# The order of scores, softmax and value products in the attention of a hybrid decoder block

## The chip, the cores and the metric

The kernel runs on one core of one Trainium2 chip. The metric is the device time of one execution in microseconds; the median over runs is compared. TensorE (PE) multiplies, VectorE (DVE), ScalarE (ACT) and GpSimd (POOL) do the rest, and SyncE (SP) issues nearly all DMA transfers.

## The reference

One decoder block on 1024 tokens of width 1024, batch 1, float32. After a norm and an input projection two branches run side by side, and a gated feed-forward layer with a short convolution follows. The change concerns the first branch, an attention with a forget gate in 8 heads of 128 channels:

```python
# log_f: log sigmoid of a forget gate, per token and head
c = jnp.cumsum(log_f, axis=1)
s = einsum('bhqd,bhkd->bhqk', q, k) * 128 ** -0.5
s = s + (c[..., :, None] - c[..., None, :])          # bias of query and key
p = softmax(where(key_pos <= q_pos, s, -inf))
y_fox = einsum('bhqk,bhkd->bhqd', p, v)
```

The second branch, a gated delta rule, is a chunked recurrence: eight chunks of 128 tokens per head, each needing the state that the one before leaves. Both branches are merged by gates, go through an output product and a norm, and then through the feed-forward layer (2816 hidden channels) and a last norm.

## The kernel before, in words

The kernel runs its stages one after the other: norm and input projection (`head_in`, `project`), the two branches together (`mix`, 812 to 1066 us in the profile), the merge (`merge`), the output product (`mix_out`), and the feed-forward layer (`ffn_up`, `ffn_down`). A float32 product is made of three: each operand is cut into a rounded high part and the rest, its low part, and high x high, high x low and low x high are summed. `split` (L106, L107) makes the parts of a tile: ScalarE casts the high part, then VectorE or GpSimd subtracts.

**Attention.** A head's 1024 queries are eight tiles of 128, numbered t; tile t sees (t + 1) x 128 keys. `probs` makes the softmax of one query tile. TensorE multiplies queries and keys into a PSUM bank (L1187 to L1189: the third pair of parts is left out). VectorE adds the bias and keeps the running maximum in one instruction (L1194), once per piece: columns left of the diagonal take the bias row `cr`, those on it the masked copy `cd`. A tile up to t = 3 is one block of scores; a later one is cut in two equal blocks. Then VectorE scales the maximum (L1200), ScalarE takes the exponential with its row sum (L1201), VectorE takes the reciprocal (L1202) and scales the row (L1203). The probabilities stay in SBUF, one tile `p0` to `p7` for each t.

`attend` makes the value products for half of the queries (512). For each key block j TensorE transposes the probability tiles that see it (L1224) into a PSUM bank, ScalarE and VectorE split the result into `ph` and `pl` (L106, L107), and three products add it up in the bank `ya` (L1215). The first half needs the probabilities of tiles 0 to 3, the second half those of tiles 4 to 7. Products run three key blocks behind the transposes.

`fox` orders the heads. For each head it goes through all score tiles, then the first half of the products, then the second. Inside the first half it starts the loads of the next head's queries and keys (`fox_load`, L1119) and its bias row (`fox_bias`, L1148 and L1150); inside the second it issues their split: `fox_query`, `fox_key` (L1135 on ScalarE, L1136 on GpSimd). Queries, keys and bias have one set of tiles in SBUF. The values of a head are loaded at the end of the head before and split by `fox_values` (L1140, L1143, L1144) after tile 4 of the scores. Head 0's tiles 0 to 3 are done early, inside the end of the projection (`fox_first`).

**What sets the order.** Each function is a generator that gives up control at each `yield`; a yield of `fox` is called a step here. A head has 26 steps (12 of scores, 5 and 9 of products), head 0 has 22. `mix` counts these steps as `i` and puts steps of the recurrence between them: `prep(h)` loads and prepares a head of the recurrence, `stream(0)` takes the even heads and `stream(1)` the odd ones, and at every odd `i` from 21 on each stream is advanced by one step. TensorE's instructions are issued in just this order. The order on the other engines and on SP is chosen by a planner that simulates the program while it is built, except for single instructions that are pinned to program order (the casts L1135 and L1143 are). Each engine, SP too, works through its queue in order, so an instruction that waits holds up those behind it.

PSUM has eight banks: in this stage four small ones, shared by scores, transposes and the recurrence (`small`), one for `ya` and three for the recurrence. SBUF pools are stacks from a left and a right end; a pool that is opened where another was closed gets its place, and its first writers wait for the last readers of the old tiles. The pool `stream2` holds the buffers `wr` through which later stages load their weights (`wload`, L126); it is opened ahead of `mix`, at the bottom of the right stack.

Of the kernel before, what the change touches and what calls it, by code (L numbers as in the profile page):

```python
# [17 lines left out]
P = 128  # L18
# [4 lines left out]
H = 8  # L23
# [64 lines left out]
class Block:  # L88
# [322 lines left out]
    def run(self):  # L411
# [5 lines left out]
        with ExitStack() as ctx:  # L417
# [30 lines left out]
            banks(4)  # L448
            self.st = pool(ctx, "stream2", side="right")
            so, sc = ExitStack(), ExitStack()  # L450
# [11 lines left out]

            self.mix([pool(left, f"fox{i}") for i in range(4)], pool(sc, "scan", side="right"), merge_pools)
            sc.close()
# [9 lines left out]
            self.merge(merge_last)  # L474
            bs.close()
            banks(2, 6)
            first = ExitStack()
# [77 lines left out]
    def head_in(self, blk, right):  # L555
# [3 lines left out]
        with tc.tile_pool(name="hin", bufs=1) as pool, ExitStack() as px:  # L559
# [96 lines left out]
            for t in range(NT):  # L656
# [12 lines left out]
                if t == NT - 2:  # L669
# [5 lines left out]
            blk.update(self.blocks(right.enter_context(tc.tile_pool(name="hnt", bufs=1, side="right", reuse_waits="tile")),  # L675
                                   ("t2", "t3", "t1")))
            scalars = self.scalars()
# [445 lines left out]

    def fox_query(self):

        self.fox_parts(self.qh, self.ql)

    def fox_key(self):
        self.fox_parts(self.kh, self.kl)

# [14 lines left out]

    def fox_bias(self, h):
        nc = self.nc
        nc.sync.dma_start(self.cr, self.rows_d[(H + h) * NT:(H + h + 1) * NT, :].rearrange("t c -> (t c)")  # L1148
                          .partition_broadcast(P))
        nc.gpsimd.affine_select(out=self.cd.rearrange("p (n c) -> p n c", n=NT),  # L1150
                                in_=self.cr.rearrange("p (n c) -> p n c", n=NT),
                                compare_op=ALU.is_ge, fill=NEG, base=0, pattern=[[0, NT], [-1, P]],
                                channel_multiplier=1)

    def fox_first(self, pool):

        self.fox_in = pool
        self.qh, self.ql, self.kh, self.kl = (pool.tile([P, S], F32R, name=n) for n in ("qh", "ql", "kh", "kl"))
        self.cr, self.cd = (pool.tile([P, S], F32, name=n) for n in ("cr", "cd"))
        self.vl = pool.tile([P, NT, P], F32R, name="vl")  # L1160
        self.fox_load(self.ql, self.q_d[0])
        self.fox_load(self.kl, self.k_d[0])
        self.fox_bias(0)
        self.fox_load_values(0)
        yield
        self.fox_query()
        yield
        self.fox_key()
        yield
        self.pts = []  # L1170
        for t in range(EARLY):
            yield from self.probs(0, t, self.pts)

    def probs(self, h, t, pts):

        nc, pool, qh, ql, kh, kl = self.nc, self.fox_in, self.qh, self.ql, self.kh, self.kl
        n = (t + 1) * P
        tsl = slice(t * P, n)
        w = n if t < 4 else n // 2
        p = (pool if t < EARLY else self.probs_pool if t < 4 else self.probs_late).tile([P, n], F32, tag=f"p{t}", name=f"p{t}")  # L1180
        mx = pool.tile([P, 4], F32, tag="mx", bufs=4, name="mx")
        top = NEG
        for lo in range(0, n, w):
            sp = self.small()
            sl = slice(lo, lo + max(w, 2 * P))
            o = sp[:, 0:sl.stop - lo]
            nc.tensor.matmul(o, qh[:, tsl], kh[:, sl], start=True, stop=False)  # L1187
            nc.tensor.matmul(o, qh[:, tsl], kl[:, sl], start=False, stop=False)
            nc.tensor.matmul(o, ql[:, tsl], kh[:, sl], start=False, stop=True)  # L1189
            for c0, c1, src in ((lo, min(lo + w, t * P), self.cr), (max(lo, t * P), lo + w, self.cd)):  # L1190
                if c0 >= c1:
                    continue
                i = (c0 > lo) + 2 * (lo > 0)
                nc.vector.tensor_tensor_reduce(p[:, c0:c1], sp[:, c0 - lo:c1 - lo], src[:, c0:c1], 1.0, top,  # L1194
                                               ALU.add, ALU.max, mx[:, i:i + 1])
                top = mx[:, i:i + 1]
            yield
        mm = pool.tile([P, 2], F32, tag="mm", bufs=4, name="mm")

        nc.vector.tensor_scalar(mm[:, 0:1], top, -QSCALE, None, op0=ALU.mult)  # L1200
        nc.scalar.activation(p, p, AF.Exp, bias=mm[:, 0:1], scale=QSCALE, accum_out=mm[:, 1:2])  # L1201
        nc.vector.reciprocal(mm[:, 1:2], mm[:, 1:2])  # L1202
        nc.vector.tensor_scalar(p, p, mm[:, 1:2], None, op0=ALU.mult)  # L1203
        pts.append(p)

    def attend(self, h, half, pts):
# [39 lines left out]
    def fox(self, pools, scan_pool):  # L1246


        self.attend_pool, self.probs_late, values, self.probs_pool = pools
        self.vh = values.tile([P, NT, P], F32R, name="vh")  # L1250
        self.vf = scan_pool.tile([P, 2, P], F32, name="vf")
        self.fox_values()
        for h in range(H):
            pts = [] if h else self.pts
            for t in range(len(pts), NT):
                yield from self.probs(h, t, pts)
                if h and t == 4:
                    self.fox_values()
            for half in range(2):
                for i, _ in enumerate(self.attend(h, half, pts)):  # L1260
                    if h + 1 < H and half == 0:
                        if i == 0:
                            self.fox_load(self.ql, self.q_d[h + 1])
                            self.fox_load(self.kl, self.k_d[h + 1])
                            self.fox_bias(h + 1)
                    elif h + 1 < H:
                        if i == 1:
                            self.fox_query()
                        elif i == 4:
                            self.fox_key()  # L1270
                    yield
            if h + 1 < H:
                self.fox_load_values(h + 1)


    def mix(self, fp, pool, before_last):
        tc, nc, a = self.tc, self.nc, self.a
        self.yf_d, self.yg_d = ([self.dr.tile([P, S], F32, name=f"{n}{h}") for h in range(H)] for n in ("yfd", "ygd"))
        if True:
# [156 lines left out]
            streams = [stream(0), stream(1)]  # L1436
            i = 0
            while take(fox, 1):
                if i in (0, 9):
                    preps[i > 0] = prep(int(i > 0))  # L1440
                if i in (0, 8, 11):
                    take(preps[0], 1)
                elif i in (9, 16, 19):
                    take(preps[1], 1)
                if i >= 21:

                    if i % 2:
# [602 lines left out]
```

## Time and profile before

| | |
|---|---|
| median of 3 runs | 1993.91 us (1989.75 to 1994.09) |
| the profiled execution | 1994.26 us, span 1992.6 us |
| mean clock granted to TensorE | 0.991 |
| TensorE busy | 1920.6 us (96%) |
| VectorE busy | 1492.4 us (75%) |
| ScalarE busy | 1067.5 us (54%) |
| GpSimd busy | 954.3 us (48%) |
| branches together (`mix`) | about 812 to 1066 us |

Times in the profile are counted from the first instruction. A row of a stretch gives the busy time of each engine in it with the number of instructions. A row of a wait reads "who waited, on which tile and line <- for whom: us in all, times, longest". Of matrix products the start is exact and the end is modelled, so the distance between starts tells what one costs when they follow each other. A waiting time put down to an engine belongs to the event that came last.

### The profile page before, as it was taken

To read this page: it belongs to the slowest core of one execution; us is meant where nothing else is said; L and a number is where in the kernel's file an instruction comes from. 1 tells how busy PE (TensorE), PEld (TensorE's weight loads), DVE (VectorE), ACT (ScalarE), POOL (GpSimd) and SP (SyncE) were. 2 spreads that over 40 slices of the span, in tenths; PEclk is the share of its full clock that TensorE was granted. 3 is DMA by queue.
4 is the path that set the end of the run, shared out by engine and by line. 5 is a ranking of instruction groups with operands and counts; after the bars stand their busy time and mean duration, and the time that the engine had idled before them with its cause. 6 is when DMAs were issued, how large, how long until landed. Compare 5 with 4: busy or idle time off the path is not lost. (4 is left out here: it accounts for less than half of the span.)

```text
span 1992.6 us, 29214 instructions
## 1 busy us (share of the span) xinstructions
PE 1920.6 (96%) x9674; PEld 1605.2 (81%) x9674; DVE 1492.4 (75%) x2549; ACT 1067.5 (54%) x2383; POOL 954.3 (48%) x792
## 2 busy tenths in 40 slices
PE   8999999999999999999998999999999999999998
PEld 8988887888887777788886887877788888877886
DVE  6949887867999974487887797668877676778435
ACT  5436776763334445476765443466555555553234
POOL 2845656555555455455655043154665656530012
PEclk9999999999999999899999999999999999999999
DMA  5335556565323366766665743573433434378654
GB/s 166 96 101 164 174 189 188 185 211 206 112 106 111 112 213 257 259 222 212 230 219 203 231 137 131 188 242 124 163 126 112 148 118 136 118 250 319 211 195 160
DMA packets 191608, 350.89 MB, mean 176 GB/s; under 512 B 50784, under 2 KB 79712, under 8 KB 191456
## 3 DMA queue, kind: packets, MB, share of 16 engines
q1 hardware_dynamic: 190448, 345.35, 51.2%
q10 hardware_dynamic: 1008, 3.67, 0.5%
q8 instruction: 76, 1.25, 0.3%
q14 instruction: 76, 0.62, 0.1%
HBM read 232.76 MB, written 116.20 MB: 175 GB/s over the span
## 5 line engine op out<-in xcount | busy, mean ns | idle before, releaser
L107 POOL TENSOR_TENSOR ol<-ws,oh 128x512 fp32r<-128x512 f32 x212 | 288.3, 1362 | 218.4 <-ACT oh L106 207.6
L107 POOL TENSOR_TENSOR ol<-wr,oh 128x512 fp32r<-128x512 f32 x165 | 230.4, 1399 | 271.0 <-ACT oh L106 213.9
L106 ACT CAST oh<-ws 128x512 fp32r<-128x512 f32 x212 | 131.0, 618 | 178.3 <-PE mm L159 172.4
L106 ACT CAST oh<-wr 128x512 fp32r<-128x512 f32 x201 | 121.5, 615 | 107.7 <-PE mm L159 74.2
L205 DVE TENSOR_TENSOR ws<-wr 128x512 f32<-128x512 f32 x106 | 99.1, 935 | 103.2 <-DMA wr<-in_w_up_dram 70.5
L390 DVE SCALAR_TENSOR_TENSOR cv<-c,fw,cv 128x512 f32<-128x512 f32 (+2 forms) x176 | 127.5, 748 | 10.0 <-ACT cv L385 8.5
L390 DVE SCALAR_TENSOR_TENSOR cv<-c,cw,cv 128x511 f32<-128x511 f32 (+2 forms) x144 | 105.9, 748 | 7.4 <-ACT cv L385 5.8
L1038 DVE TENSOR_TENSOR invt<-invz 128x399 f32<-128x399 f32 (+50 forms) x114 | 94.7, 845 | 0.3
L264 ACT COPY x<-mm 128x512 f32<-128x512 f32 x158 | 91.7, 581 | 4.5 <-PE mm L159 4.5
L159 PE MATMUL mm<-b22h,oh 128*128 128x512 f32 x216 | 86.1, 399 | 7.4 <-ACT x L264 7.3
L159 PE MATMUL mm<-bt1h,oh 128*128 128x512 f32 x216 | 85.2, 395 | 5.1 <-ACT x L264 5.1
L107 DVE TENSOR_TENSOR ol<-wd,oh 128x512 fp32r<-128x512 f32 x66 | 46.3, 706 | 57.5 <-ACT oh L106 57.4
L159 PE MATMUL mm<-bt4h,oh 128*128 128x512 f32 x216 | 84.8, 393 | 4.4 <-DVE c L311 4.4
L159 PE MATMUL mm<-b11h,ol 128*128 128x512 f32 x216 | 86.2, 399 | 0.7 <-POOL ol L107 0.7
L159 PE MATMUL mm<-b11h,oh 128*128 128x512 f32 x216 | 85.8, 397 | 1.0 <-ACT oh L106 1.0
L159 PE MATMUL mm<-b11l,oh 128*128 128x512 f32 x216 | 86.4, 400 | 0.0
L159 PE MATMUL mm<-b22l,oh 128*128 128x512 f32 x216 | 86.0, 398 | 0.0
L159 PE MATMUL mm<-b21l,oh 128*128 128x512 f32 x216 | 86.0, 398 | 0.0
L159 PE MATMUL mm<-bt4l,oh 128*128 128x512 f32 x216 | 85.7, 397 | 0.0
L159 PE MATMUL mm<-bt2l,oh 128*128 128x512 f32 x216 | 85.1, 394 | 0.3 <-DVE bt2l L107 0.3
L159 PE MATMUL mm<-bt1l,oh 128*128 128x512 f32 x216 | 84.9, 393 | 0.0
L159 PE MATMUL mm<-b21h,oh 128*128 128x512 f32 x216 | 84.9, 393 | 0.0
(426 smaller groups left out, 6381.0 us busy)
## 6 DMA issues: line engine op xcount, KB each, us to landing
wr<-in_w_up_dram SPq DMA_DIRECT2D x43, 512.0 KB, 3.6
wr<-in_w_gdn_dram SPq DMA_DIRECT2D x24, 512.0 KB, 3.8
wr<-in_w_out_dram SPq DMA_DIRECT2D x24, 512.0 KB, 3.9
s<-hy SPq DMA_DIRECT2D x44, 256.0 KB, 3.0
s<-z SPq DMA_DIRECT2D x44, 256.0 KB, 3.9
wd<-in_w_down_dram SPq DMA_DIRECT2D x44, 256.0 KB, 5.7
b22h<-s SPq DMA_DIRECT2D x44, 256.0 KB, 2.9
b22l<-s SPq DMA_DIRECT2D x44, 256.0 KB, 3.3
```

The source lines that it names most:

```text
L106: cast = nc.scalar.copy(hi, src)
L107: (lo_eng or nc.vector).tensor_tensor(lo, src, hi.bitcast(F32), ALU.subtract)
L159: self.nc.tensor.matmul(ps, lhs[:, sl], rhs[:, k, :], start=(first and k == 0 and i == 0), stop=(k == 3 and i == 2), skip_group_check=True)
L205: v.tensor_tensor(t, x, y, op)
L264: nc.scalar.copy(t, x)
L390: nc.vector.scalar_tensor_tensor(t[:, lo:], c[:, 512 * j + lo - s:512 * (j + 1) - s], w[:, n - 1 - s:n - s], t[:, lo:], op0=ALU.mult, op1= ...
L1038: nc.vector.tensor_tensor(tv, z[:, m:n, 0:n].to_broadcast([P, r, n]), z[:, m, c0:c1].unsqueeze(2).to_broadcast([P, r, n]), ALU.mult))
```

## The change

The change has these parts.

1. `fox` no longer goes through scores, first half and second half in turn. For each head a list gives the order of 26 steps: four times (one step of the first half's products, two score steps of tiles 4 to 7), then the rest of the first half, and the second half's products with the four score tiles 0 to 3 of the next head between them. Since tiles 0 to 3 of a head are always done ahead, as head 0's already were, the first step of each head is a step of products.
2. There are two sets of tiles for queries, keys and the bias row of the first 512 keys (`fox_set`), used by heads in turn. The loads for the next head go out at step 1 of a head, the splits of its queries and keys are issued at steps 6 and 8, that of the head's own values at step 4.
3. The bias row and its masked copy are made in two halves of 512 keys (`fox_bias(h, half)`); the second half's tiles are shared by all heads, and its load goes out after step 12.
4. Scores go in blocks of 512 keys rather than equal halves: tile 4 has now 512 and 128 columns (the second is computed 256 wide), tile 5 512 and 256, tile 6 512 and 384, tile 7 512 and 512 as it was.
5. A score tile of one block gives up control after its softmax rather than before it.
6. `mix` starts the first recurrence head ahead of the first attention step, and the following ones two to three steps earlier.
7. The pool `stream2` is opened after the merge rather than ahead of `mix`, which makes room for the second set; the tiles `t1`, `t2`, `t3` of the projection are laid out in another order.

```diff
-            self.st = pool(ctx, "stream2", side="right")
             so, sc = ExitStack(), ExitStack()
...
-            self.mix([pool(left, f"fox{i}") for i in range(4)], pool(sc, "scan", side="right"), merge_pools)
+            self.mix([pool(left, f"fox{i}") for i in range(5)], pool(sc, "scan", side="right"), merge_pools)
...
             self.merge(merge_last)
             bs.close()
+            self.st = pool(ctx, "stream2", side="right")
...
-                                   ("t2", "t3", "t1")))
+                                   ("t1", "t2", "t3")))
...
+    def fox_bias(self, h, half):
+        nc, n = self.nc, NT // 2
+        cr, cd = self.bias(h, half)
+        r0 = (H + h) * NT + half * n
+        nc.sync.dma_start(cr, self.rows_d[r0:r0 + n, :].rearrange("t c -> (t c)").partition_broadcast(P))
+        nc.gpsimd.affine_select(out=cd.rearrange("p (n c) -> p n c", n=n), in_=cr.rearrange("p (n c) -> p n c", n=n),
                                 compare_op=ALU.is_ge, fill=NEG, base=0, pattern=[[0, n], [-1, P]],
                                 channel_multiplier=1)
+    def bias(self, h, half):
+        return (self.crh if half else self.sets[h % 2][4]), self.cd[half]
+
+    def fox_set(self, pool):
+        return ([pool.tile([P, S], F32R, name=n) for n in ("qh", "ql", "kh", "kl")]
+                + [pool.tile([P, 512], F32, name="crl")])
+
+    def fox_load_head(self, h):
+        _, ql, _, kl, _ = self.sets[h % 2]
+        self.fox_load(ql, self.q_d[h])
+        self.fox_load(kl, self.k_d[h])
+        self.fox_bias(h, 0)
...
     def probs(self, h, t, pts):
...
-        w = n if t < 4 else n // 2
...
-        for lo in range(0, n, w):
+        for half, lo in enumerate(range(0, n, 512)):
             sp = self.small()
-            sl = slice(lo, lo + max(w, 2 * P))
+            hi = min(lo + 512, n)
+            sl = slice(lo, max(hi, lo + 2 * P))
...
-            yield
+            if hi < n:
+                yield
...
         pts.append(p)
+        yield
...
     def fox(self, pools, scan_pool):
...
+            late, early = late(), early()
+            order = [first, late, late] * 4 + [first, early, early, early, last, last, last, early] + [last] * 6
+            for i, part in enumerate(order):
+                if i == 0:
+                    if h == 0:
+                        self.fox_values()
+                elif i == 1 and more:
+                    self.fox_load_head(h + 1)
+                elif i == 4 and h:
                     self.fox_values()
+                elif more and i == 6:
+                    self.fox_query(h + 1)
+                elif more and i == 8:
+                    self.fox_key(h + 1)
+                if next(part, DONE) is not DONE:
                     yield
+                if i == 12:
+                    finish(first)
+                    if more:
+                        self.fox_bias(h + 1, 1)
+            for part in (first, late, early, last):
+                finish(part)
+            if more:
                 self.fox_load_values(h + 1)
+            pts = after
...
     def mix(self, fp, pool, before_last):
...
+            preps[0] = prep(0)
+            take(preps[0], 1)
             while take(fox, 1):
-                if i in (0, 9):
-                    preps[i > 0] = prep(int(i > 0))
-                if i in (0, 8, 11):
+                if i == 6:
+                    preps[1] = prep(1)
+                if i in (5, 8):
                     take(preps[0], 1)
-                elif i in (9, 16, 19):
+                elif i in (6, 14, 17):
                     take(preps[1], 1)
-                if i >= 21:
+                if i >= 19:
...
-                elif i >= 12 and i % 2:
+                elif i >= 9 and i % 2:
                     take(streams[0], 1)
```

More of the change, by code (lines that the diff above doesn't have):

```diff
@@ L1122, in fox_load_values, with fox_query, fox_key @@
         self.fox_load(self.vl, self.vd[:, h * P:(h + 1) * P].rearrange("(t p) d -> p t d", p=P))
[L1124 to L1129, printed above, removed]
+    def fox_query(self, h):
+        self.fox_parts(*self.sets[h % 2][0:2])
+    def fox_key(self, h):
+        self.fox_parts(*self.sets[h % 2][2:4])
     def fox_parts(self, hi, lo):
@@ L1144, in fox_values @@
             self.nc.gpsimd.tensor_tensor(self.vl[:, sl], raw[:, sl], self.vh[:, sl].bitcast(F32), ALU.subtract)
[L1146 to L1152, printed above, removed]
-                                channel_multiplier=1)
+    def fox_bias(self, h, half):
[4 more added lines that the diff above has]
+        nc.gpsimd.affine_select(out=cd.rearrange("p (n c) -> p n c", n=n), in_=cr.rearrange("p (n c) -> p n c", n=n),
+                                compare_op=ALU.is_ge, fill=NEG, base=0, pattern=[[0, n], [-1, P]],
+                                channel_multiplier=1)
@@ L1155, in fox_first @@
+    def bias(self, h, half):
[8 more added lines that the diff above has]
+        self.fox_bias(h, 0)
     def fox_first(self, pool):
         self.fox_in = pool
-        self.qh, self.ql, self.kh, self.kl = (pool.tile([P, S], F32R, name=n) for n in ("qh", "ql", "kh", "kl"))
@@ L1159, in fox_first @@
-        self.cr, self.cd = (pool.tile([P, S], F32, name=n) for n in ("cr", "cd"))
+        self.sets = [self.fox_set(pool)]
+        self.crh = pool.tile([P, 512], F32, name="crh")
+        self.cd = [pool.tile([P, 512], F32, name=f"cd{i}") for i in range(2)]
         self.vl = pool.tile([P, NT, P], F32R, name="vl")
-        self.fox_load(self.ql, self.q_d[0])
-        self.fox_load(self.kl, self.k_d[0])
-        self.fox_bias(0)
+        self.fox_load_head(0)
         self.fox_load_values(0)
+        self.fox_bias(0, 1)
@@ L1165, in fox_first @@
         yield
-        self.fox_query()
+        self.fox_query(0)
         yield
-        self.fox_key()
+        self.fox_key(0)
         yield
@@ L1174, in probs @@
     def probs(self, h, t, pts):
-        nc, pool, qh, ql, kh, kl = self.nc, self.fox_in, self.qh, self.ql, self.kh, self.kl
+        nc, pool, (qh, ql, kh, kl, _) = self.nc, self.fox_in, self.sets[h % 2]
         n = (t + 1) * P
         tsl = slice(t * P, n)
-        w = n if t < 4 else n // 2
-        p = (pool if t < EARLY else self.probs_pool if t < 4 else self.probs_late).tile([P, n], F32, tag=f"p{t}", name=f"p{t}")
+        p = (pool if t < EARLY else self.probs_late).tile([P, n], F32, tag=f"p{t}", name=f"p{t}")
         mx = pool.tile([P, 4], F32, tag="mx", bufs=4, name="mx")
-        top = NEG
-        for lo in range(0, n, w):
+        top, i = NEG, 0
+        for half, lo in enumerate(range(0, n, 512)):
             sp = self.small()
-            sl = slice(lo, lo + max(w, 2 * P))
+            hi = min(lo + 512, n)
+            sl = slice(lo, max(hi, lo + 2 * P))
             o = sp[:, 0:sl.stop - lo]
@@ L1189, in probs @@
             nc.tensor.matmul(o, ql[:, tsl], kh[:, sl], start=False, stop=True)
-            for c0, c1, src in ((lo, min(lo + w, t * P), self.cr), (max(lo, t * P), lo + w, self.cd)):
+            cr, cd = self.bias(h, half)
+            for c0, c1, src in ((lo, min(hi, t * P), cr), (max(lo, t * P), hi, cd)):
                 if c0 >= c1:
                     continue
-                i = (c0 > lo) + 2 * (lo > 0)
-                nc.vector.tensor_tensor_reduce(p[:, c0:c1], sp[:, c0 - lo:c1 - lo], src[:, c0:c1], 1.0, top,
+                nc.vector.tensor_tensor_reduce(p[:, c0:c1], sp[:, c0 - lo:c1 - lo], src[:, c0 - lo:c1 - lo], 1.0, top,
                                                ALU.add, ALU.max, mx[:, i:i + 1])
-                top = mx[:, i:i + 1]
-            yield
+                top, i = mx[:, i:i + 1], i + 1
+            if hi < n:
+                yield
         mm = pool.tile([P, 2], F32, tag="mm", bufs=4, name="mm")
@@ L1246, in fox @@
     def fox(self, pools, scan_pool):
-        self.attend_pool, self.probs_late, values, self.probs_pool = pools
+        self.attend_pool, self.probs_late, values, other, _ = pools
         self.vh = values.tile([P, NT, P], F32R, name="vh")
         self.vf = scan_pool.tile([P, 2, P], F32, name="vf")
-        self.fox_values()
+        self.sets.append(self.fox_set(other))
+        pts = self.pts
         for h in range(H):
[L1254 to L1257, printed above, removed]
-                    self.fox_values()
[L1259 to L1270, printed above, removed]
-                    yield
-            if h + 1 < H:
@@ new lines, in fox, with late, early @@
+            more, after = h + 1 < H, []
+            first, last = self.attend(h, 0, pts), self.attend(h, 1, pts)
+            def late():
+                for t in range(4, NT):
+                    yield from self.probs(h, t, pts)
+            def early():
+                for t in range(4 if more else 0):
+                    yield from self.probs(h + 1, t, after)
+            late, early = late(), early()
+            order = [first, late, late] * 4 + [first, early, early, early, last, last, last, early] + [last] * 6
```

## The prediction

> **What bounds the kernel now.** I read the page first, then the table of stretches, the waits of TensorE, and the order of time around two heads.
>
> ```profile
> PE 1920.6 (96%) x9674; PEld 1605.2 (81%) x9674; DVE 1492.4 (75%) x2549; ACT 1067.5 (54%) x2383; POOL 954.3 (48%) x792
> ```
>
> TensorE is busy for 96% of the span, so a change can give back only the time in which it waits, or runs at a lower clock. The change touches the attention stage alone. The next rows are the first head there, then the sum over the six heads from 843.0 to 1036.4 us, then the last head (columns: stretch, its length, busy time of each engine, granted clock, DMA share, GB/s; a sum row ends in means).
>
> ```profile
> 811.90:843.00 31.10, 27.13 (x178) 22.86 (x176) 18.94 (x54) 15.11 (x34) 15.66 (x14) 0.84 0.97 334
> sum 193.42, PE 182.70 PEld 166.59 DVE 156.62 ACT 134.67 POOL 112.95; mean PE 30.45 PEld 27.77 DVE 26.10 ACT 22.44 POOL 18.82
> 1036.40:1065.40 29.00, 26.79 (x189) 24.11 (x187) 22.65 (x87) 22.00 (x69) 9.98 (x12) 1.00 0.39 135
> ```
>
> Six heads take 193.4 us, 32.2 each, of which TensorE idles 10.7 in all. The first head loses 31.1 - 27.1 = 4.0 us idle, and its mean clock of 0.84 costs up to 0.16 x 31.1 = 5.0 more. The last head idles 2.2. These 21.9 us are the ceiling. VectorE has 26.1 us of work in a head of 32.2: enough room over a head, if it is spread. It isn't: one head, cut where the last score goes out.
>
> ```profile
> 904.36:918.00 13.64, 12.72 (x91) 11.88 (x89) 12.93 (x57) 9.73 (x35) 4.89 (x5) 1.00 0.47 142
> 918.00:937.30 19.30, 17.98 (x135) 15.80 (x135) 13.39 (x38) 13.18 (x40) 10.10 (x9) 1.00 0.95 316
> ```
>
> While TensorE does scores, VectorE is busy for 12.9 of 13.6 us; in the value products for 13.4 of 19.3. It still falls behind, as three moments of this head show (start, length, engine, line):
>
> ```profile
> 916.38 0.40 PE L1189 MATMUL ms<-kh,ql 128*128 128x512 f32 x1
> 923.97 0.75 DVE L1203 TENSOR_SCALAR p<-p,mm 128x1024 f32<-128x1024 f32 x1
> 924.78 0.33 PE L1224 MATMUL ms<-ident,p 128*128 128x128 f32 x1 [0.71 <-DVE p L1203]
> ```
>
> The last score is issued at 916.4, its tile is normalised 7.6 us later, and the transpose that needs it waits. TensorE's waits in the six heads say the same (us in all, times, longest):
>
> ```profile
> PE ya L1215 <- DVE pl L107: 3.7, 3, 2.0
> PE ms L1224 <- DVE pl L107: 1.8, 3, 1.2
> PE ms L1224 <- DVE p L1203: 1.8, 3, 0.7
> PE ms L1224 <- DVE mx L1194: 1.0, 1, 1.0
> ```
>
> 8.3 of the 10.7 us are waits for VectorE.
>
> **The change, part by part.** *Order of scores and products.* A head has 26 steps of TensorE: 12 of scores, then 14 of products. Afterwards the first twelve hold the eight score steps of tiles 4 to 7 and four steps of the first half; the other fourteen the rest of the products and the four early tiles of the next head. What this does to VectorE comes from these rows (the first is L1194 alone, the rest groups over the six heads; us in all, mean ns):
>
> ```profile
> 843.00:1036.00 193.00, 48.16 (x228) 1.00 0.63 214
> L1203 DVE TENSOR_SCALAR p<-p,mm 128x128 f32<-128x128 f32 (+7 forms) x48 | 34.0, 708 | 0.1
> L1202 DVE RECIPROCAL mm<-mm 128x1 f32<-128x1 f32 x48 | 7.3, 153 | 0.7 <-ACT p L1201 0.6
> L1200 DVE TENSOR_SCALAR mm<-mx 128x1 f32<-128x1 f32 x48 | 6.6, 140 | 0.1
> L107 DVE TENSOR_TENSOR pl<-ms,ph 128x512 fp32r<-128x512 f32 (+2 forms) x60 | 35.7, 605 | 12.9 <-ACT ph L106 12.3
> ```
>
> Softmax costs VectorE (48.16 + 34.0 + 7.3 + 6.6) / 6 = 16.0 us a head, the low parts of the transposed tiles 35.7 / 6 = 5.95. Of 26.1 that leaves 4.2 for the scans (overlaps counted off), by steps 1.9 in twelve and 2.3 in fourteen. The early tiles have 1280 of 4608 columns (28%, 4.4 us) and half of the tiles (8.0 us); I take 5.0, nearer the columns, since most of L1203 and L1194 grows with width. The first half has 10 of 36 transposes: 1.65 of 5.95. So the score steps hold now 16.0 + 1.9 = 17.9 us of VectorE against 12.7 of TensorE, an excess of 5.2; afterwards 11.0 + 1.65 + 1.9 = 14.5, an excess of 1.8 (TensorE's 12.7 left as it is: the early scores leave, transposes and two products come). The fourteen others get 5.0 + 4.3 + 2.3 = 11.6 against some 18. If waits shrink with the excess, 1.8 / 5.2 = 35% stays: **-7.0 us** of 10.7 in six heads, **-1.4** of 2.2 in the last. Ends: nothing, and all 12.9.
>
> *The start.*
>
> ```profile
> 811.90:828.50 16.60, 13.55 (x79) 10.70 (x78) 12.60 (x42) 7.60 (x16) 7.22 (x6) 0.80 0.95 361
> 820.90 0.41 PE L1224 MATMUL ms<-ident,p 128*128 128x128 f32 x2 [1.06 <-DVE mx L1194]
> 822.24 0.48 PE L1224 MATMUL ms<-ident,p 128*128 128x128 f32 x1 [0.93 <-DVE pl L107]
> 823.37 0.63 PE L1215 MATMUL ya<-ph,vl 128*128 128x512 f32 x1
> 816.99 1.10 SPq L126 DMA_DIRECT2D wr<-in_w_out_dram  x2
> ```
>
> Head 0 has the same eight score steps and four of products in its first 16.6 us, with 12.6 of VectorE in them. These stay; TensorE's four transposes can now fill the gaps, so at best the stretch shrinks to 12.6: **-4.0 us**, between nothing and the whole 9.0. Waits of about 1 us were enough here for half speed: 823.37 follows at 0.42 us spacing and longer. The Trainium skill ("TensorE: Matmul & The Clock Gate", Part 1) has the clock fall after an idle window of about 3.4 us; no wait here is that long, so the trace does not agree. By that rule only the 4.0 idle us are to be had, at the same share 1.8, and the sum would be 2.2 smaller.
>
> *Blocks of 512 keys.* Tile 4 goes from 320 + 320 to 512 + 256 columns; the others keep theirs.
>
> ```profile
> 915.92 0.39 PE L1187 MATMUL ms<-kh,qh 128*128 128x512 f32 x1
> 916.15 0.40 PE L1188 MATMUL ms<-kl,qh 128*128 128x512 f32 x1
> ```
>
> 512 columns go out every 0.23 us, so 128 more in three products cost 0.17 us, in eight heads **+1.4**. VectorE loses one reduction of 192 columns a head (in the excess above, under 0.4 us; not counted).
>
> *Second set of queries and keys.* These loads had to wait on SP for the last scores, and now need not:
>
> ```profile
> SPq L1119 <- PE ms L1188: 27.9, 5, 8.9
> ```
>
> No TensorE wait in the six heads names them, so I cost this at nothing; it is the condition for the new order. Their casts stay pinned on ScalarE, from steps 18 and 21 to 6 and 8; behind them stand the exponentials and the high parts of the transposes.
>
> *Bias by halves.* One more 256 KB load and one more select a head; POOL's select of 1024 columns (below) costs between the same and twice as much: 0 to 1.1 us a head on an engine busy 18.8 of 32.2. Nothing on the path.
>
> *The weight stream's tiles* (three loads of 512 KB that went out at 817.0) open after the merge. They leave the start's full DMA (share 0.97; part of the start's bounds) and enter the merge, long before the output product at about 1250. I take 0. If they delay the merge's loads, 1.5 MB at the 334 GB/s above is +4.7; that is the upper end. The reorder of three tiles moves addresses alone: 0.
>
> **Sum:** -7.0 - 1.4 - 4.0 + 1.4 = -11.0. The profiled execution took 1994.3 us (span 1992.6), 0.4 over the median, so 1983.3. Ends: -21.9 + 1.4, 1973.8; and 0 + 1.4 + 4.7, 2000.4. For the forecast itself, 1977 to 1988.
>
> **Rivals.** *VectorE stays the bound.* POOL's low parts come under the late normalisations now:
>
> ```profile
> 914.57 2.55 POOL L1144 TENSOR_TENSOR vl<-vl,vh 128x512 fp32r<-128x512 f32 x2 [5.59 <-ACT vh L1143]
> 915.93 1.53 DVE L1203 TENSOR_SCALAR p<-p,mm 128x640 f32<-128x640 f32 x1
> 919.85 0.60 DVE L1203 TENSOR_SCALAR p<-p,mm 128x768 f32<-128x768 f32 x1
> ```
>
> 640 columns took 1.53 us beside POOL, 768 took 0.60 without. If all four late tiles pay 0.93, that is 3.7 us a head; the mean of 708 ns over the eight widths, against about 0.45 at 0.60's pace, shows some 1.0 paid already on four. With 2.7 more the excess is 4.5 of 5.2, 87% of each wait stays, and the sum is -0.13 x (12.9 + 4.0) + 1.4 = -0.8: 1993.5. Against it: VectorE's own order is chosen by a planner, not by the file. The Trainium skill ("SBUF — State Buffer", Who interferes with whom) states the rule behind this: VectorE and GpSimd share a port pair under an exclusive lock, and the later one blocks wholly. The rows agree. The planner could also keep VectorE's old order, and then the change doesn't do what it says; the time is the same.
>
> *More than forecast:* all waits and the lost clock go, 1974 to 1977. For it: the fourteen other steps have over 6 us of spare VectorE. Against it: some waits are chains, not load.
>
> *Slower: the next head's low parts come late.* Place: the first early score, at step 13. The key's low part starts after step 8, behind the values' and the query's, in the same twelve steps:
>
> ```profile
> L1144 POOL TENSOR_TENSOR vl<-vl,vh 128x512 fp32r<-128x512 f32 x12 | 16.4, 1383 | 19.1 <-ACT vh L1143 19.0
> L1136 POOL TENSOR_TENSOR ql<-ql,qh 128x512 fp32r<-128x512 f32 x12 | 15.2, 1287 | 8.5 <-ACT qh L1135 8.5
> L1136 POOL TENSOR_TENSOR kl<-kl,kh 128x512 fp32r<-128x512 f32 x12 | 15.2, 1287 | 1.7 <-ACT kh L1135 1.7
> L1150 POOL TENSOR_SCALAR_AFFINE_SELECT cd<-cr 128x1024 f32<-128x1024 f32 x6 | 6.6, 1094 | 19.5 <-DMA cr<-rows 19.5
> ...
> 782.82 0.39 PE L1188 MATMUL ms<-kl,qh 128*128 128x256 f32 x1 [2.77 <-POOL kl L1136]
> ```
>
> That is (16.4 + 15.2 + 15.2 + 6.6) / 6 = 8.9 us of POOL in a burst, with waits for loads between. A step takes 32.2 / 26 = 1.24 us, so from step 8 to 13 there are 6.2 us; it decides when the key's low part ends later than that. Such a wait costs 2.77 us (head 0's first score); in seven heads 19.4, and -11.0 + 19.4 gives 2002.7. Against it: the old order left four steps after the key's cast, the new one five, without such a wait between heads.
>
> **How the numbers follow.** Forecast 0.40; more than forecast 0.14; VectorE stays the bound, 1988 to 2000, 0.26; late low parts, above 2000, 0.20. 0.3% (6 us) is about what a measurement of this kernel can tell from no change: below 1988 is faster, 0.40 + 0.14 + 0.02 of the third = 0.56; 0.24 the same; 0.20 slower. The range leaves out 0.03 below 1975 and 0.15 above 2003.
>
> **What would show it.** Right: the stretch from the first transpose to the last value product falls by 8 to 14 us, VectorE's busy share becomes even over a head, waits of L1224 and L1215 for L107, L1203 and L1194 fall below 6 us, and TensorE's clock near 820 to 830 is above 0.8. Wrong: L1203's mean grows well over 708 ns; L1188 or L1215 wait for POOL; the merge after 1066 waits longer for its loads.

## The result, and the profile after

The changed kernel takes **2025.62 us** (median of four runs, 2023.3 to 2029.17), the kernel before 1992.18 on the same occasions: ratio 1.017, 95% interval 1.0149 to 1.0191. It is slower by some 33 us, and the predicted range ended at 2003.

The profiled execution took 2025.05 us, span 2023.3, 30.8 us more than that of before. The page's first part (busy time, share, instructions) already says that the number of products did not grow: 9674 as before, which take 10 us longer.

```profile
PE 1930.7 (95%) x9674; PEld 1611.0 (80%) x9674; DVE 1489.6 (74%) x2533; ACT 1072.0 (53%) x2383; POOL 961.1 (48%) x800
```

The attention stage is cut here in three, in both kernels at the same events: its start, the eviction of the second half's sums (`ye`) of head 0, that of head 6, and the merge's first product. The columns are those of the prediction's stretches. After:

```profile
811.00:848.50 37.50, 31.89 (x211) 27.33 (x210) 26.04 (x83) 20.25 (x54) 18.30 (x17) 0.86 1.00 325
848.50:1067.10 218.60, 192.69 (x1383) 172.80 (x1382) 156.57 (x540) 135.64 (x433) 113.66 (x124) 0.95 0.56 184
1067.10:1097.70 30.60, 24.80 (x152) 22.27 (x150) 19.91 (x56) 20.57 (x57) 13.60 (x16) 0.89 0.26 87
```

Before:

```profile
811.90:843.80 31.90, 27.93 (x184) 23.66 (x183) 19.25 (x55) 15.61 (x36) 16.46 (x15) 0.84 0.95 327
843.80:1037.20 193.40, 182.68 (x1380) 166.57 (x1379) 156.69 (x553) 134.56 (x432) 112.15 (x120) 1.00 0.64 215
1037.20:1067.70 30.50, 26.24 (x182) 23.38 (x180) 24.41 (x90) 23.90 (x75) 10.38 (x14) 1.00 0.41 135
```

The stage is 286.7 us long instead of 255.8, which is the whole difference. The six heads in the middle have nearly the same work (tile 4's blocks are wider) and take 25.2 us more. TensorE idles 25.9 us in them instead of 10.7, and its products take 10.0 us longer, at a mean granted clock of 0.95. The first stretch now holds the early tiles of head 1 as well, and the last one lacks such tiles, so these two are compared together: 68.1 against 62.4 us.

TensorE's waits in the six heads after (us in all, times, longest):

```profile
PE ya L1232 <- ACT vh L1143: 11.7, 3, 6.5
PE ya L1232 <- POOL vl L1144: 5.4, 4, 1.5
PE ms L1204 <- POOL ql L1136: 4.8, 1, 4.8
PE ms L1203 <- POOL kl L1136: 2.0, 1, 2.0
PE us L1386 <- DVE sr L1383: 0.9, 3, 0.4
PE us L1381 <- DVE ss L1398: 0.8, 1, 0.8
```

VectorE, which 8.3 us of waits named before, is down to 1.7 us. In its place stand 17.1 us for the parts of the **values** (L1143 is the cast to the high part, L1144 the subtraction of the low part) and 6.8 us for those of queries and keys. The last two rows are products of the recurrence.

The longest of them, in order of time. TensorE (start, length, engine, line):

```profile
990.34 0.39 PE L1232 MATMUL ya<-pf,vf 128*128 128x128 f32 x2
...
999.33 0.27 PE L1241 MATMUL ms<-ident,p 128*128 128x128 f32 x1
1006.05 0.80 PE L1232 MATMUL ya<-ph,vh 128*128 128x512 f32 x1 [6.45 <-ACT vh L1143]
1006.64 0.63 PE L1232 MATMUL ya<-pl,vh 128*128 128x512 f32 x1
```

SP's queue at that time, and ScalarE's cast:

```profile
989.55 0.47 SPq L1320 DMA_DIRECT2D sat<-a21d  x1
...
994.78 0.63 SPq L1320 DMA_DIRECT2D sqd<-qdd  x1
995.52 0.56 SPq L1261 DMA_DIRECT2D yfd<-ye  x1
996.21 0.37 SPq L1119 DMA_DIRECT2D vl<-vd  x1
```

```profile
1005.38 1.14 ACT L1143 CAST vh<-vl 128x512 fp32r<-128x512 f32 x2 [2.65 <-DMA vl<-vd]
```

At a head's last product, 990.3, the one tile of the loaded values is free. The load of the next ones goes out at 996.2, behind ten loads of the recurrence and a store; ScalarE has them at 1005.4, and the next head's first product follows at 1006.1. TensorE was ready for it at 999.6, 9.3 us after the last product. In the old order the same chain had more room (TensorE and SP, before):

```profile
937.15 0.39 PE L1215 MATMUL ya<-pf,vf 128*128 128x128 f32 x2
954.00 0.47 PE L1215 MATMUL ya<-ph,vh 128*128 128x512 f32 x1
```

```profile
936.49 0.38 SPq L1119 DMA_DIRECT2D vl<-vd  x1
```

There the first product came 16.9 us after the last. By steps: the old order has 15 from a head's last product to the next one's first (twelve of scores, then three key blocks of transposes), the new one nine. The chain of 990.3 to 1006.1 took 15.7 us; it fits into the one and not into the other.

That is the longest of the three waits for the cast, and the only one that ends on the load. In head 1 the load went out at 847.9 and landed 8.0 us later, when TensorE was ready (856.2); but ScalarE had an exponential and the cast of the next head's key ahead, and cast the values at 859.7, which made TensorE wait for 4.2 us. In head 6 the data were there at 1036.5 and the cast came at 1042.4, behind an exponential, copies and half of the key's cast; the wait was 1.05 us. In heads 3 and 4 the values were in time. So ScalarE's order belongs to the chain too.

The second kind of wait, on GpSimd (start, length) with TensorE's row behind it:

```profile
895.99 2.82 POOL L1144 TENSOR_TENSOR vl<-vl,vh 128x512 fp32r<-128x512 f32 x2
...
900.93 2.52 POOL L1136 TENSOR_TENSOR kl<-kl,kh 128x512 fp32r<-128x512 f32 x2
903.40 2.42 POOL L1422 TENSOR_TENSOR so<-so,srs 128x512 f32<-128x512 f32 x2
905.88 0.52 POOL L1342 MEMSET sxt<- 64x512 f32 x1
906.48 2.82 POOL L1136 TENSOR_TENSOR ql<-ql,qh 128x512 fp32r<-128x512 f32 x2
```

```profile
908.12 0.58 PE L1204 MATMUL ms<-kh,ql 128*128 128x256 f32 x1 [4.75 <-POOL ql L1136]
```

GpSimd works through values, key and query and the recurrence's own tiles without a gap, and the first early score stands for 4.75 us: the slower rival's wait, at its place. It comes in two of the six heads, here for the query and once, 2.0 us, for the key, and in head 0 (2.8 us).

### The profile page after: what moved, and what is told of

The parts are those of the page before. It is cut to its first block, busy times and chain, and to the rows that moved or that the text cites. A ratio compares the mean times of both kernels' runs of the same rounds, so it can differ in the third digit from the quotient of the medians.

```text
span 2023.3 us, 29182 instructions
## 1 busy us (share of the span) xinstructions
PE 1930.7 (95%) x9674; PEld 1611.0 (80%) x9674; DVE 1489.6 (74%) x2533; ACT 1072.0 (53%) x2383; POOL 961.1 (48%) x800
## 5 line engine op out<-in xcount | busy, mean ns | idle before, releaser
L159 PE MATMUL mm<-bt2h,oh 128*128 128x512 f32 x216 | 84.4, 391 | 1.8 <-ACT x L264 1.8
```

Of the source, the lines that this page charges most:

```text
L159: self.nc.tensor.matmul(ps, lhs[:, sl], rhs[:, k, :], start=(first and k == 0 and i == 0), stop=(k == 3 and i == 2), skip_group_check=True)
```

## The experiments

Theory A: what costs is the values. One buffer, free only after a head's last product, must be loaded and split in nine steps. Theory B, the prediction's slower rival: the burst of low parts on GpSimd. Theory C: something else of the change. Ratios are to the kernel before on the same chip; what an edit gives back is counted as the difference of two ratios, 0.1% being 2 us, and is uncertain by some 6 us where four runs were made. One kernel's runs spread over 10 us (the kernel before: 1989.2 to 1999.4 in 13), and in the traces the stage starts between 805.5 and 816.4 us though the edits hardly touch the code ahead of it. So the stage's own length in the trace is given beside the time: 286.7 us after, 255.8 before. Line numbers move by a few lines from kernel to kernel.

**The old order.** The changed kernel with the old order of steps, and with the steps of loads and splits that suit it; everything else as changed.

```diff
-            order = [first, late, late] * 4 + [first, early, early, early, last, last, last, early] + [last] * 6
+            order = [late] * 8 + [first] * 5 + [last] * 9 + [early] * 4
```

(loads at step 8, values split at 2, query and key at 14 and 17)

> The changed kernel with the list of steps put back to the order of the kernel before: eight score steps of tiles 4 to 7, five steps of the first half, nine of the second, then the four early tiles of the next head; loads at step 8, values' parts at step 2, queries' and keys' parts at steps 14 and 17. Two sets of queries and keys, bias by halves, blocks of 512 and the later weight pool stay. If the new order of steps is what costs (first theory), the time comes back to 1990 to 1998 us. If the rest of the change costs (other addresses, weight pool, blocks, bias loads), it stays above 2010.

2000.6 us, ratio 1.0027 (1.0013 to 1.0041), stage 261.0 us: just above the first theory's range and far below the other's. The order and the places of loads and splits that go with it cost some 28 of the 33 us. One new wait stood out:

```profile
PE ms L1360 <- DMA sx<-xd: 5.5, 1, 5.5
```

It is TensorE, in the first head, on a load of the recurrence. It comes back below.

**A second tile for the loaded values.** The load goes out at step 1 of the head before; the cast stays at step 4.

```diff
-        self.vl = pool.tile([P, NT, P], F32R, name="vl")
+        self.vls = [pool.tile([P, NT, P], F32R, name="vl")]
...
+        self.vls.append(more_values.tile([P, NT, P], F32R, name="vl2"))
```

> The changed kernel with a second tile for the raw values and their low part, loaded at step 1 of the head before with the queries and keys; the high part and the step of its cast (4) stay. Theory A (the values' chain: one buffer that is free only after the last product of the head before, then load, cast and subtraction within nine steps): the waits of the value products for the high and low part, 17 us in the changed kernel, fall below 5, and the time to 1995 to 2005. Theory B (GpSimd's burst of parts in the first twelve steps is what is late, whatever the load): the waits for the low parts of values, queries and keys stay, and the time stays above 2012.

2021.65 us, 1.0136 (1.0111 to 1.0161), stage 282.8 us. TensorE's waits in the stage:

```profile
PE ms L1204 <- POOL kl L1136: 11.4, 4, 4.8
PE ms L1205 <- POOL ql L1136: 4.7, 1, 4.7
...
PE ya L1233 <- ACT vh L1144: 1.0, 1, 1.0
PE ya L1233 <- POOL vl L1145: 1.0, 1, 1.0
```

The waits for values are gone, 2.0 us of 17.1, and those for query and key have grown from 9.6 (in the whole stage) to 16.1. So the waits go as theory A says, and the time as theory B. TensorE now reaches the early scores sooner, and GpSimd has not finished: a wait removed uncovers the one behind it.

**Two whole sets of values**, split at step 14 of the head before, away from the burst (`ph` and `pl` with three buffers instead of four, for room).

```diff
+                    self.fox_load_values(h + 1)
+                elif more and i == 14:
+                    self.fox_values(h + 1)
-                elif i == 4 and h:
-                    self.fox_values()
```

> The changed kernel with two whole sets of values (raw and low, high, last block), loaded at step 1 and split at step 14 of the head before; to make room, three buffers rather than four for the split transposes. Theory A: no value product waits for its values, and the time is 1985 to 2000. Theory B: GpSimd has the same work in a head, but the values' part has left the first twelve steps, so the waits for the low parts of queries and keys (9.6 us) fall too, to the same 1985 to 2000; if value waits move into others, 2005 and more.

2011.25 us, 1.0082 (1.0053 to 1.0111), stage 271.4 us; slower than either theory's 1985 to 2000. No product waits for values, and the low parts of query and key still cost 12.6 us:

```profile
PE ms L1204 <- POOL kl L1136: 9.5, 4, 3.5
...
PE ms L1205 <- POOL ql L1136: 3.1, 1, 3.1
```

Theory A alone is worth some 18 us by the ratios, 15 by the stage.

**The values' low part on VectorE** instead of GpSimd: GpSimd's burst is 2.7 us shorter in every head, the values' load no earlier.

```diff
-            self.nc.gpsimd.tensor_tensor(self.vl[:, sl], raw[:, sl], self.vh[:, sl].bitcast(F32), ALU.subtract)
+            self.nc.vector.tensor_tensor(self.vl[:, sl], raw[:, sl], self.vh[:, sl].bitcast(F32), ALU.subtract)
```

> The changed kernel with the subtraction that makes the values' low part on VectorE rather than GpSimd. Theory A: the wait for the high part (11.7 us, cast on ScalarE after the load) stays, only the wait for the low part (5.4 us) goes: 2012 to 2022. Theory B: GpSimd's queue is 2.7 us a head shorter where it is late, so waits for queries' and keys' low parts (9.6 us) fall as well: below 2010.

2025.02 us, 1.0162 (1.0122 to 1.0201): no change that the runs can tell, and outside both ranges. The four runs spread from 2021.0 to 2036.2, and the trace is that of the slowest, so its waits are not those of the median. In it the waits for GpSimd fall and the one for the cast grows:

```profile
PE ya L1232 <- ACT vh L1143: 14.3, 3, 9.1
...
PE ms L1203 <- POOL kl L1136: 3.0, 2, 2.8
```

**Queries and keys two heads ahead**, values as in the changed kernel: loads at step 13 of the head before last, splits at 18 and 21 (the masked bias of the first half moves with them).

```diff
+                if h + 2 < H and i == 13:
+                    self.fox_load_parts(h + 2)
+                if h + 2 < H and i == 18:
+                    self.fox_query(h + 2)
+                if h + 2 < H and i == 21:
+                    self.fox_bias(h + 2, 0)
+                    self.fox_key(h + 2)
```

> The changed kernel with only the queries and keys of the next head but one loaded at step 13 and split at steps 18 and 21; the values keep their one buffer and step 4. Theory B: with 5.2 us less of parts in GpSimd's first twelve steps the values' low part comes earlier too; the waits for values fall below 6 and the time to 1995 to 2008. Theory A: values still wait for their load and cast, more than 10 us: 2008 to 2018.

2006.84 us, 1.0064 (1.0041 to 1.0087), stage 271.7 us, so B alone is worth some 21 us by the ratios, 15 by the stage. The time is in theory B's range, but the waits for values do not fall below 6 us as it had them; the one for the cast stays, somewhat smaller, with 1.9 us more for their low part:

```profile
PE ya L1235 <- ACT vh L1143: 9.1, 2, 7.7
```

**Both**: two sets of values and queries and keys two heads ahead.

> As the kernel with two whole sets of values, and the next head but one's queries and keys are loaded at step 13 and split at steps 18 and 21, a whole head before they are used; the new order of steps stays. Theory B (GpSimd's parts come too late in the first twelve steps): the waits for the low parts of queries and keys, 12.6 us there, fall below 4 (head 0's first score keeps its 2.8), and the half clock behind them goes: 1988 to 1998 us. If something else bounds the new order (VectorE, the port, the recurrence), the time stays above 2003.

2006.92 us, 1.0069 (1.0041 to 1.0096). Better than the changed kernel by some 20 us, no better in time than the step before, and not the 1988 to 1998 expected. Yet its stage is 264.2 us long, 7.5 less than in the step before; that one's trace reaches the stage at 808.1 and this one's at 813.4 us. Four runs each can't tell whether the second edit gains 7 us or nothing. Its six middle heads, cut as above, and TensorE's main waits in them:

```profile
853.20:1046.20 193.00, 184.20 (x1383) 166.14 (x1382) 156.37 (x540) 131.94 (x429) 107.75 (x122) 1.00 0.68 219
```

```profile
PE us L1398 <- DVE mm L1220: 1.6, 2, 0.9
PE ms L1245 <- DVE mm L1220: 1.4, 1, 1.4
PE us L1393 <- ACT so L1415: 1.2, 2, 0.8
PE ms L1372 <- DMA sx<-xd: 1.2, 1, 1.2
PE us L1407 <- DVE yge L1446: 0.9, 1, 0.9
```

All waits for parts are gone, the clock is full, and the six heads take 193.0 us against 193.4 before. This is the new order without what went wrong in it, and **it gains 0.4 us of the 7.0 forecast**. TensorE idles 8.8 us there instead of 10.7, and its products take 1.5 us more. VectorE still ends 5.9 us of the waits (9.3 before, the prediction's 8.3 and two smaller rows): they now fall on the recurrence's products too (L1398, L1407 among them). The old order with the change's small parts (the last experiment below) is the nearer comparison, and its six heads are no longer:

```profile
850.70:1043.60 192.90, 184.92 (x1381) 166.48 (x1381) 155.45 (x544) 134.03 (x432) 112.25 (x125) 1.00 0.65 210
```

There VectorE ends 7.1 us of the waits. So in these heads no gain of the order can be told from none. (The kernel with both has three buffers for the split transposes instead of four; what that costs was not run alone.)

The loss that is left lies at the two ends: the stage runs from 813.4 to 1077.6 us, 264.2 long, so its first and last stretch have 71.2 us against 62.4.

**The ends.** The kernel with both, with the old order in the first and last head, in the first only, and in the last only. In the first two, head 1's early tiles take the masked bias of head 2, which is written before they run: the work is the same, the result is not, and the tiles also wait for that row.

```diff
+            if h in (0, H - 1):
+                order = [late] * 8 + [first] * 5 + [last] * 9 + [early] * 4
```

> The kernel with all parts split ahead (2006.9 us), with the first and the last head in the order of before (all scores, then all products; the next head's early tiles last) and the six heads between in the new order. Nothing is left out. Theory (what that kernel still loses, it loses at both ends of the stage, where the new order has no neighbouring head to draw work from): its start idles 7.6 us and loses 5.1 to the clock in 31.6 us, before's start 4.0 and 5.0 in 31.1; its last stretch idles 7.8 and loses 1.6, before's 4.3 and nothing. With both ends as before, 3.5 + 5.1 = 8.6 us go: 1998.3 (1995 to 2001.5). Rival (the new order costs in the middle heads, or in the stages before and behind): the time stays at 2003 to 2010.

> As the kernel with all parts split ahead, but only the first head in the order of before. Theory of the ends: 3.5 us less than 2006.9: 2003.4 (2001 to 2005.5). If the whole of the rest lies in the first head, 1995 to 1999; if it lies in the last, 2006 to 2009.

> As the kernel with all parts split ahead, but only the last head in the order of before. Theory of the ends: 5.1 us less than 2006.9: 2001.8 (1999 to 2004). The wait for the last tile's softmax (3.1 us, then half clock for 5 us) should go down to the 0.7 us of before, since five steps of the first half stand behind the last score instead of one. Rival (the last scores come no earlier, so the wait only moves): 2005 to 2008.

2004.88 us (1.0067, 1.0045 to 1.0089), 2007.54 (1.0076, 1.0058 to 1.0094) and 2002.03 (1.0047, 1.003 to 1.0063). The first is in the rival's range, the second where the whole rest would lie in the last head. The third is in the theory's, but its interval overlaps that of the kernel without this edit, and its trace (of its slowest run, 5.2 us over the median) doesn't bear the reason out: the wait for the last tile's softmax is gone, another has come, and the merge starts at 1078.1 instead of 1077.6 us. Its waits in the stage:

```profile
PE ms L1206 <- DVE mx L1213: 3.4, 1, 3.4
PE a L1667 <- ACT yh L106: 3.4, 1, 3.4
PE ms L1441 <- POOL so L1436: 3.2, 2, 3.1
PE ms L1207 <- POOL kl L1136: 2.8, 1, 2.8
```

Where the rest is lost is seen, then: at the ends. That the order there causes it is not shown, and the traces speak against it: the first stretch, 39.8 us with everything split ahead, is 39.4, 39.0 and 39.8 us in these three, the last, 31.4, is 31.9, 31.4 and 31.8. At the start VectorE itself waits, here in the kernel with both:

```profile
818.49 0.69 DVE L1213 CUSTOM_DVE_ANT_0 p<-ms,crl 128x512 f32<-128x512 f32 x1 [4.14 <-DMA gtd<-c]
```

The profile puts this wait down to the store of a tile `c` that the end of the projection writes. It stands in the changed kernel (2.3 us), in all but one of those built from it with the new order, and in the two with the first head in the old order (4.2 and 5.1 us); it doesn't stand in the kernel before, in the two built from that, or in the two with the old order in all heads. That fits a pool that got the place of `c` and whose first writer has to wait; no run tested it.

**The small parts.** The kernel before with the weight pool opened after the merge, and the kernel before with blocks of 512 keys:

```diff
             bs.close()
+            self.st = pool(ctx, "stream2", side="right")
             banks(2, 6)
```

> The kernel before with one part of the change: the weight pool is opened after the merge. As predicted, 0: 1990 to 1998 and no interval off 1. If the places that this moves make the first recurrence head's loads wait (5.5 us in the kernel with the old order), 1998 to 2003.

1991.22 us, ratio 0.9984 (0.9969 to 1.0), stage 252.6 us.

```diff
-        for lo in range(0, n, w):
+        for lo in range(0, n, 512):
             sp = self.small()
+            w = min(512, n - lo)
```

> The kernel before with one part of the change: scores by blocks of 512 keys. As predicted +1.4 us for the wider tile 4, so 1992 to 1999, a ratio of 1.0007.

1996.65 us, ratio 1.0011 (0.9999 to 1.0024), stage 258.1 us. Its six heads have 2.0 us more of TensorE work than those of before (184.70 for 182.68) in 192.5 us, and it has a wait of its own:

```profile
847.60:1040.10 192.50, 184.70 (x1381) 165.98 (x1380) 154.26 (x540) 134.62 (x434) 112.77 (x119) 1.00 0.64 216
```

```profile
PE ms L1325 <- DMA sx<-xd: 6.8, 1, 6.8
```

**The old order with the old steps of the recurrence too**, so that the second set, the bias by halves, the blocks and the pool are left of the change, with the two small parts (the place of one `yield` and the order of `t1` to `t3`).

```diff
-                if i == 6:
-                    preps[1] = prep(1)
+                if i in (0, 9):
+                    preps[i > 0] = prep(int(i > 0))
```

> The changed kernel with the old order of scores and products (as in the first experiment, 2000.6 us) and with the old step numbers of the scans as well, so that what is left of the change is the second set of queries and keys, the bias by halves, the blocks of 512 keys and the later weight pool. Nothing is left out. In the first experiment one wait stood out, TensorE on a load of the scans at the start (5.5 us, L1360 for sx). Theory (this wait came from the scans' earlier steps, and the rest of the change is worth nothing): 5.5 us less, 1992 to 1997, ratio 0.998 to 1.002, and the wait goes back to the 0.9 us of before. Rival (the second set's loads, which no longer wait for the last scores, take the DMA time or SP's turn from the scans' loads): the wait stays at 3 us or more, 1998 to 2002.

1998.13 us, 1.0016 (1.0005 to 1.0026), stage 259.5 us, and the wait is not smaller but larger:

```profile
PE ms L1360 <- DMA sx<-xd: 7.3, 1, 7.3
```

So it did not come from the recurrence's earlier steps. That it comes from the second set's loads isn't shown either: the kernel with blocks of 512 alone has one set and 6.8 us of the same wait. What they share is a start in which DMA is full (share 0.97 in the prediction's row). The load takes 9 to 11 us to its use in the kernel before and in these two (issued at 823.7, 825.7 and 826.8, used at 834.4, 835.6 and 835.7). TensorE was ready for it at 833.5 before, and at 828.8 and 828.4 in these: it got there sooner, and the wait is longer, but the first of its products starts 22.4 to 22.9 us after the start of the stage in all three. What the longer wait brings is a slower clock behind it: the sixteen products of this line take 1.9 us instead of 1.0. None of these versions beats the kernel before by more than its interval; the nearest is the late weight pool, 0.9984.

## Why the prediction was wrong

**The step that failed** is the one on the second set of queries and keys: "I cost this at nothing; it is the condition for the new order". It priced the loads by the waits of the old order ("No TensorE wait in the six heads names them") and asked of none of a head's three operands how long before its first use its tile comes free in the new order. The sum has no term for the values at all. Their first product moved from 15 steps behind the last of the head before to nine, 16.9 to 9.3 us in the traces, under a chain (queue, load, ScalarE's turn, cast) of up to 15.7 us. That cost 17.1 us of waits in the six heads, with 6.8 us for query and key; the half clock behind them made the products 8.5 us longer than the same number takes in the kernel with everything split ahead (192.7 against 184.2).

**Order of scores and products, -7.0 and -1.4.** The second step that failed. Waits for VectorE in the six heads fell from 9.3 us (8.3 in the rows shown) to 1.7, but while TensorE stood elsewhere. Where nothing else is late (both parts ahead) they are 5.9 us and the heads take 0.4 us less; with the old order and the same small parts they are 7.1 us and the heads take as long (192.9). "If waits shrink with the excess" should have left 35% of them; some 60% stayed, on the recurrence among others, whose work the step took for spread evenly and harmless. The last stretch got no shorter (30.6 us for 30.5), though it had lost a head's early tiles to the one before.

**The start, -4.0.** Wrong in sign: first and last stretch together are 5.7 us longer, 8.8 with both parts ahead. The first head now has the key of head 1 to wait for (2.8 us), VectorE stands for the store named above (2.3 us), and the prediction's reason, that transposes fill the gaps of the softmax, had no run of its own: the two with the old order in the first head did not get the loss back.

**Blocks of 512, +1.4.** In range: +2.2 us, interval -0.2 to 4.8. The interval holds zero too, and the trace doesn't show the term by itself: its six heads idle 2.9 us less than before's, and its start has the wait of 6.8 us.

**Weight pool, 0.** Right within 0.3%: -3.2 us, interval -6.2 to 0. The upper end of +4.7 is excluded.

**Second set and bias by halves, 0 each.** With the old order all small parts together give +3.2 us (1.0 to 5.2). With -3.2 for the pool and +2.2 for the blocks, some 4 us are left for these two, with an uncertainty as large: not told from zero, nor from each other.

**Rivals.** *VectorE stays the bound* through GpSimd's port: no, the normalisation became cheaper, not dearer than 708 ns. VectorE in the six heads after:

```profile
L1219 DVE TENSOR_SCALAR p<-p,mm 128x640 f32<-128x640 f32 (+7 forms) x48 | 31.6, 658 | 0.3
```

But its price was nearly right for the order itself, 0.4 us gained instead of 7.0, which is luck: the mechanism that it priced did not show. (Its working also takes some 1.0 us a head as paid already; 708 less 450 ns on eight tiles is 2.1.) *Slower, low parts late*: right in kind and place, and the reason given against it ("the old order left four steps after the key's cast, the new one five") did not hold, since values and the other of the two stood ahead on GpSimd. Its 19.4 us (2.77 us in seven heads) is near what query and key ahead alone gave back, 21 by the ratios and 15 by the stage, but by luck: the traced waits are three, 9.6 us in all, and the rest is the clock and shorter waits for the values. The time was missed because the values came on top. The gains don't add up: by the ratios 7 us for a second tile, 18 for two sets, 21 for query and key, 20 for both; by the stages 4, 15, 15 and 22.5. Of the things named to show it wrong, the waits of scores and products for POOL appeared; the wait of L1232 for ScalarE's cast was not on the list.

**What stays open:** why the two ends cost 9 us more with everything split ahead (the store at the start is a reason that the trace offers, not one that was tested), what three buffers cost, and whether the order gains anything where nothing is late.

## What to carry to other kernels

When steps are reordered, write down for each operand when its buffer comes free and when it is first used, in the old and the new order, and set the time between beside its whole chain as the trace shows it: queue, transfer, the turn on the engine that casts, cast, subtraction. An operand that no wait names today may have hidden in the order that is being removed. And where one engine's waits are to go, see which engine will end the next wait before booking them as gain.

## What the runs showed of the hardware

The same load does not always take the same time. The six loads of the values, 512 KB each, landed 3.7 to 9.1 us after their issue, the median being 4.8. The slowest was also issued 5.9 us after the head's last product, behind ten loads and a store that SP sent in the 6.7 us ahead of it.

The longest wait cost twice. The 6.45 us are followed by two products 0.59 us apart (1006.05 and 1006.64 above); the same two of an undisturbed group are 0.32 apart (988.22 and 988.54). Two stretches, just ahead of its end and behind it:

```profile
1004.00:1006.00 2.00, 0.00 (x0) 0.00 (x0) 0.00 (x0) 0.62 (x2) 2.00 (x3) 0.50 1.06 334
1006.00:1010.00 4.00, 2.43 (x5) 1.62 (x6) 0.00 (x0) 0.52 (x2) 3.90 (x4) 0.50 0.14 23
```

TensorE's granted clock is 0.50 before it starts again and for the 4 us behind. The Trainium skill ("TensorE: Matmul & The Clock Gate", Part 1) says that after an idle window of about 3.4 us the clock is halved until TensorE has been busy for about as long. For this wait the trace agrees; for the start of the kernel before, where waits of about 1 us were followed by half speed, it did not. Over the six heads this second cost was some 8.5 us (against the kernel with everything split ahead) beside 15.2 us more of idling.
